# Seven-product matmuls of an fp32 macaron block: a merge with seven additions and a seeded PSUM bank, plain weight sums, one sum per block by an adding DMA, four quads in every gate/up block

## The chip, the cores and the metric

The kernel runs on one core of a Trainium2 chip. The metric is the device time in microseconds (us) of one execution; the number for a kernel is the median of its runs.

## The reference, cut to what matters

A block of width 2048 on 256 positions, all in fp32: half a feed-forward network (FFN1), a hybrid mixer (RWKV7 scan, pooling branch, gates), and half a second feed-forward network (FFN2), each with an RMS norm before and after. What the change touches is the two FFNs and, by the same functions, the mixer's last matmul.

```python
D_MODEL, SEQ, D_FF = 2048, 256, 5632      # D_FF = ceil(8 * 2048 / 3 / 256) * 256

def _swiglu(x, w_gate, w_up, w_down):
    return (jax.nn.silu(x @ w_gate) * (x @ w_up)) @ w_down
...
f = _swiglu(_rmsnorm(h, ln_ffn1_pre), ffn1_gate, ffn1_up, ffn1_down)
h = h + 0.5 * _rmsnorm(f, ln_ffn1_post)
mx = _hybrid_mixer(_rmsnorm(h, ln_mix_pre), ...)       # ends in m @ w_out
h = h + _rmsnorm(mx, ln_mix_post)
f = _swiglu(_rmsnorm(h, ln_ffn2_pre), ffn2_gate, ffn2_up, ffn2_down)
h = h + 0.5 * _rmsnorm(f, ln_ffn2_post)
```

## The kernel before, in words

**Precision.** A matmul in fp32 is made of three in fp32r: every operand is split into a high part (a cast on ACT) and a low part (the difference, on DVE), and `mm3` (L317) adds aH bH, aH bL and aL bH in one PSUM bank; its lines L319, L320, L321 are the three matmuls. The 256 positions are two halves h of 128, the weights come in tiles of 128 rows (k tiles) by 512 columns.

**A weight pair** (`fetch`, L362) is two k tiles: SP loads 512 KB into a w32 buffer, ACT casts it into a wH buffer of a ring of five (L373), DVE makes the low part wL (L383, 128 x 1024), PE uses it for 2 k tiles x 2 halves x 3 = 12 matmuls, and the ring buffer comes free.

**The seven-product scheme.** `seven` (L508) multiplies two weight blocks of 512 columns with the same activations: f and l are gate and up of the same columns, or two column blocks of down or of w_out. It takes a string of letters. `f` and `l` are a pair of that block. `q`, a quad, takes two k tiles of both blocks at once and makes the 2 x 2 products of them with seven multiplications in place of eight, so 21 matmuls for 24. For that, DVE makes sums of the raw weights: t13 (L576, 1024 wide), t2 (L581) and t4 (L585, 512 wide each), and four low parts (L598: three of 1024 and one of 512). The sums of the activations (S, L441 to L446) are made once per FFN and used by all blocks. The results collect in eight PSUM banks: f0, f1, l0, l1 (pool "mm", four buffers) also take the pairs' products; p1, p5, p6, p7 (pool "ms", four buffers) take only quads.

**The merge.** After a block's last quad ACT copies p1 into a buffer u0 (L640), and DVE makes u1 = p6 + u0, u2 = p7 + u1, u1 = p5 + u1 and u3 = p5 + u2, four additions of 512 that each read the one before or its neighbour (L645, `u<-ms`). When the f pairs are through, `close_f` adds f0 and f1 (L645, `u<-mm`), and at the block's end `total` (L693) adds l0 and l1: eight additions.

**The stages of an FFN.** `ffn` (L989) runs over 11 column blocks of gate and up. The first is multiplied without `seven`, the second with pairs only, and the other nine by turns with four quads ("ffqfqfqlqlll") and three ("fffqffqlqllll"): 32 quads. Silu of gate on ACT (L1067) times up on DVE (`mult`, L1074) gives the block of h, which DVE transposes in 32 x 32 pieces (L875), POOL moves by DMA (L892, `x<-T`), and ACT and DVE split into high and low (`carry`, L932; the lows are L909). Then `post` runs down: four column blocks in two calls of `seven`, the second of which holds back 16 k tiles of one block (TRAIL) and multiplies them at the end, first for one half of the positions, then for the other (`by_half`, L402). At the very end each half is squared and summed (in down by a custom DVE instruction, L1173, after `total`; in the mixer's w_out stage by ACT straight from the bank, L987), POOL takes the root (L1178), and DVE scales and adds the residual (L1182).

**The order.** The program writes the order of every engine by hand. A planner (`Plan.solve`, L137) places the operations with list scheduling: PE's sequence is given by the code; every operation has a due time, worked back from its first use on PE with planned latencies (LAT), and of those that can start first on an engine the one due first goes ahead. Loads may start at most FETCH = 22 us before they are due.

Of the kernel before, what the change touches and what calls it, by code (L numbers as in the profile page):

```python
# [47 lines left out]
GATE_UP = ["", "ffffffffllllllll"] + ["ffqfqfqlqlll", "fffqffqlqllll", "ffqfqfqlqlll", "fffqffqlqllll", "ffqfqfqlqlll", "fffqffqlqllll", "ffqfqfqlqlll", "fffqffqlqllll", "ffqfqfqlqlll"]  # L48
SUMS = (2, 2)
BY_DMA = range(0)  # L50
LAT = dict(PE=0.22, DVE=0.1, ACT=0.17, SP=0.0, POOL=8.0)
# [169 lines left out]
class Block:  # L221
# [95 lines left out]
    def mm3(s, ps, aH, aL, bH, bL, start, stop):  # L317
        nc = s.nc
        nc.tensor.matmul(ps, aH, bH, start=start, stop=False)  # L319
        nc.tensor.matmul(ps, aH, bL, start=False, stop=False)  # L320
        nc.tensor.matmul(ps, aL, bH, start=False, stop=stop)  # L321
# [99 lines left out]
    def sums(s, T, Td, j, out, own=None, nq=2, used=(), x32=None):  # L421
# [13 lines left out]
        def second():  # L435
            x = tt["x"] if x32 is None else x32[0][0].rearrange(
                "p (a b) t -> p a b t", b=2)[:, :nq]
            a11, a21 = x[:, :, 0, :P], x[:, :, 0, P:]
            a12, a22 = x[:, :, 1, :P], x[:, :, 1, P:]
            f = tt["f"] = s.unit((P, 4, nq, P), F32, "sf")  # L440
            V.scalar_tensor_tensor(out=f[:, 0], in0=a21, scalar=-1.0, in1=a22, op0=ALU.mult,  # L441
                                   op1=ALU.subtract)
            V.scalar_tensor_tensor(out=f[:, 1], in0=f[:, 0], scalar=-1.0, in1=a11,
                                   op0=ALU.mult, op1=ALU.subtract)
            V.tensor_tensor(out=f[:, 2], in0=a11, in1=a21, op=ALU.subtract)
            V.tensor_tensor(out=f[:, 3], in0=a12, in1=f[:, 1], op=ALU.subtract)  # L446
# [61 lines left out]
    def seven(s, wf, cf, wl, cl, at, dep, KT, need, sm, order, ev_f, ev_l, used, trail=0):  # L508
# [4 lines left out]
        n = order.count("q")  # L513
# [4 lines left out]
        left = dict(f0=std + n, f1=std, l0=std + n, l1=std + n, p1=n, p5=n, p6=n, p7=n)  # L518
# [9 lines left out]
        def mul(b, x, wt):  # L528
# [5 lines left out]
            s.mm3(bank[b], *x, *wt, new, left[b] == 0)  # L534
# [9 lines left out]
        def pair(k, w, c0, b, by_dma):  # L544
            low, dst = s.fetch(w, k, c0, keep, by_dma, by_dma)

            def do():
                for i in range(2):
                    for h in range(2):
                        mul(f"{b}{h}", rows(k + i, h), ws[k + i])  # L550
            d = p.pe(12 * MM, do, [low, dep(k)] + claim(b + "0", b + "1"), dst)
# [3 lines left out]
        def quad(q):  # L555
# [10 lines left out]
            def get(m):  # L566
                i, x_ = m // 2, "ab"[m % 2]
                if m < 2:
                    v[x_] = raw((ka, kb)[m])
                w, c0 = ((wl, cl), (wf, cf))[(m + i) % 2]  # L570
                nc.sync.dma_start(out=v[x_][:, i],
                                  in_=w[(k + i) * P:(k + i + 1) * P, c0:c0 + 512])

            def t13():
                v["t13"] = s.unit((P, 2, 512), F32, "t13")
                V.tensor_tensor(out=v["t13"], in0=v["a"],  # L576
                                in1=v["b"][:, :1].to_broadcast([P, 2, 512]), op=ALU.subtract)
# [6 lines left out]
            def t4():  # L584
                V.tensor_tensor(out=v["t24"][:, 1], in0=v["b"][:, 1], in1=v["t24"][:, 0],  # L585
                                op=ALU.subtract)
# [9 lines left out]
            def low(n_, m):  # L596
# [3 lines left out]
            ld = [p.op("SP", 0.4, lambda m=m: get(m), take=([ka], [kb], (), ())[m], size=0.26,  # L600
                       chain="SP", ahead=FETCH) for m in range(4)]

            def half(n_, m, deps, rel):
# [5 lines left out]
            n13 = p.op("DVE", two, t13, ld[:3], [k13, k24], [ka, kb])  # L609
            la, ra = half("a", 2, [ld[0], ld[2]], [ka])  # L610
            n2 = p.op("DVE", one, t2, [n13], (), [ka, k13])
# [7 lines left out]
                                  mul("f0", S_(4), x["a"][1])),  # L619
                 [la, ds, dep(k)] + claim("p1", "f0", "f1"), ra)  # L620
            p.pe(3 * MM, lambda: mul("l0", rows(k + 1, 0), x["b"][0]),
                 [lb] + claim("l0", "l1"), rb)
# [4 lines left out]
                                      mul("l1", rows(k + 1, 1), x["t24"][1])),  # L627
# [14 lines left out]
        def add(o, b, i):  # L642
            if u[o] is None:
                new(o)
            V.tensor_tensor(out=u[o], in0=bank[b], in1=u[i], op=ALU.add)  # L645
        m, use = {}, {}

        def merge(d):
            for i in range(4):
# [4 lines left out]
            for o, b, i in ((1, "p6", 0), (2, "p7", 1), (1, "p5", 1), (3, "p5", 2)):  # L654
                d = m[f"u{o}"] = p.op("DVE", one, lambda o=o, b=b, i=i: add(o, b, i),
                                      [d] + (use[o][0] if o > 1 or b == "p6" else []))
                held[b].append(d)
                use[i][1].append(d)
        nq, last = 0, {}
        ks = dict(f=iter(range(K0, KT, 2)), l=iter(range(K0, KT - trail, 2)))  # L660
        for c in order:
            if c == "q":
                last["q"] = quad(nq)
# [10 lines left out]
            if c == "f" and left["f"] == std // 2:  # L674
                m["f"] = last["f"]

                def close_f():
                    for h, i in ((0, 1), (1, 3)):
                        if n:
                            d = p.op("DVE", one, lambda h=h, i=i: add(i, f"f{h}", i),  # L680
                                     [last["f"], m[f"u{i}"], last["q"]])
# [5 lines left out]
                if not n or "u3" in m:  # L687
# [4 lines left out]
        def total(h):  # L692
            V.tensor_tensor(out=u[2 * h], in0=bank[f"l{h}"], in1=u[2 * h], op=ALU.add)  # L693
        if trail:
            def finish(h, d):
                d = p.op("DVE", one, lambda: total(h), [d, m["u0"], m["u3"]], due=p.clk)
                ev_l(h, d, lambda: u[2 * h], None)
            s.by_half(wl, cl, KT - trail, KT, lambda k, h: mul(f"l{h}", rows(k, h), ws[k]),
                      keep, finish, [dep(k) for k in range(KT - trail, KT, 4)],
                      used)  # L700
            return
        for h in range(2):
            if n:
                d = p.op("DVE", one, lambda h=h: total(h), [p.last, m["u0"], m["u3"]])
                held[f"l{h}"].append(d)
                ev_l(h, d, lambda h=h: u[2 * h], use[2 * h][1])
# [282 lines left out]
    def ffn(s, wg, wu, wd, uT, rs, gpost, resid, emit, reload, xs=None):  # L989
# [53 lines left out]
        su, sud, suk = [None] * 4, {}, []  # L1043
# [96 lines left out]
    def post(s, wd, at, KT, gpost, fac, resid, emit, reload, hT, hTd, sm, plan, hTk=None):  # L1140
# [8 lines left out]
        part, direct = [None, None], KT == NKD  # L1149
# [865 lines left out]
```

## Time and profile before

| | before |
|---|---|
| median of 3 runs | 2017.59 us (2016.92 to 2018.37) |
| span of the profiled execution | 2015.4 us |
| time of the profiled execution itself | not listed apart; the span is 2.2 us under the median |
| PE busy | 2000.9 us (99%) |
| DVE busy | 1824.7 us (91%) |
| ACT busy | 1192.3 us (59%) |
| POOL busy | 327.6 us (16%) |
| HBM read | 396.69 MB, 201 GB/s over the span |

The span is the time between the first and the last record of one execution under the profiler. A busy time adds the durations of an engine's instructions; matmuls overlap their neighbours (one lasts 0.39 us, the next starts 0.23 us after it), so that PE's rate is read from the distance of starts. A row of a timeline is start, length, engine, line, operation, output<-input, shapes and how many in a row; in square brackets stands how long the engine was idle before it, and for whom. A row of groups gives count, busy time, mean ns of one, and idle time before.

### The profile page before, as it was taken

The numbers are of one execution on the slowest core, as the hardware profiler recorded it, in microseconds if no ns is written. First come the engines' busy times: TensorE is split into PE (matmuls) and PEld (weight loads), VectorE is DVE, ScalarE is ACT, GpSimd is POOL, SyncE is SP. The second block draws the span as 40 slices with busy tenths as digits, with TensorE's granted clock in tenths as the row PEclk, the third lists the DMA queues.
The fourth block names the chain that finished last, engine by engine and source line by source line (L and its number), as shares of the span: only waits on it lengthen the run. The fifth ranks groups of instructions, "written<-read, shape, count | busy, mean of one in ns | idle before, by whom it ended". The sixth has DMA issues, their size and how long they took to land.

```text
span 2015.4 us, 28684 instructions
## 1 busy us (share of the span) xinstructions
PE 2000.9 (99%) x9957; PEld 1655.1 (82%) x9957; DVE 1824.7 (91%) x2424; ACT 1192.3 (59%) x1586; POOL 327.6 (16%) x673
## 2 busy tenths in 40 slices
PE   9999999999999999999999999999999999999997
PEld 7888888888888888888788788888888888888886
DVE  6999999999999957789689678979999999999997
ACT  7555665556666566685476434665656555566663
POOL 0111211131000123403220111011113111310000
PEclk9999999999999999999999999999999999999999
DMA  7675674667568577757456547666656747665683
GB/s 268 224 241 182 220 242 160 218 213 241 175 203 299 209 212 214 205 175 214 146 173 190 159 168 269 244 216 215 228 198 218 245 142 235 211 228 183 207 294 126
DMA packets 227419, 423.56 MB, mean 210 GB/s; under 512 B 24639, under 2 KB 28105, under 8 KB 227273
## 3 DMA queue, kind: packets, MB, share of 16 engines
q1 hardware_dynamic: 204713, 384.70, 57.9%
q0 software_dynamic: 22272, 36.51, 5.5%
q8 instruction: 78, 1.28, 0.3%
q10 hardware_dynamic: 288, 0.52, 0.1%
q14 instruction: 68, 0.56, 0.1%
HBM read 396.69 MB, written 8.39 MB: 201 GB/s over the span
## 4 chain that ended last, share of the span: by engine, by line
PE 97%; DVE 1%; issue 1%; DMA 0%; ACT 0%; POOLq 0%; POOL 0%; DVEq 0%; ACTq 0%
PE mm L319 27%; PE mm L321 26%; PE mm L320 26%; PE ms L320 5%; PE ms L321 5%; PE ms L319 5%; PE tr L849 1%; PE pA L1733 0%; DVE u L645 0%; PE mc L817 0%; DMA x<-in_x_dram 0%; PE pU L1829 0%; PE pSa L1841 0%; PE pY L1864 0%; PE pT L1900 0%
## 5 line engine op out<-in xcount | busy, mean ns | idle before, releaser
L319 PE MATMUL mm<-wH,xH 128*128 128x512 f32 (+1 forms) x2116 | 825.5, 391 | 0.0
L320 PE MATMUL mm<-wL,xH 128*128 128x512 f32 (+1 forms) x2116 | 821.2, 388 | 0.0
L321 PE MATMUL mm<-wH,xL 128*128 128x512 f32 (+1 forms) x2116 | 821.1, 388 | 0.0
L319 PEld LDWEIGHTS mm<-wH,xH 128*128 128x128 f32 x2116 | 397.4, 188 | 82.1
L321 PEld LDWEIGHTS mm<-wH,xL 128*128 128x128 f32 x2116 | 397.4, 188 | 82.0 <-DVE xL L867 0.2
L373 ACT CAST wH<-w 128x1024 fp32r<-128x1024 f32 x313 | 326.2, 1054 | 231.7 <-PE mm L321 208.1
L320 PEld LDWEIGHTS mm<-wL,xH 128*128 128x128 f32 x2116 | 397.7, 188 | 79.7
L383 DVE TENSOR_TENSOR wL<-w,wH 128x1024 fp32r<-128x1024 f32 x313 | 373.0, 1218 | 18.9 <-ACT wH L373 17.3
L593 ACT CAST wH<-t 128x1024 fp32r<-128x1024 f32 x208 | 219.4, 1055 | 217.0 <-PE mm L321 108.9
L296 DVE TENSOR_TENSOR wL<-w,wH 128x1024 fp32r<-128x1024 f32 (+2 forms) x200 | 236.6, 1192 | 95.7 <-ACT wH L295 94.1
L295 ACT CAST wH<-w 128x1024 fp32r<-128x1024 f32 (+2 forms) x200 | 205.4, 1034 | 170.9 <-PE mm L321 150.7
L892 POOL DMA_DIRECT2D x<-T x352 | 173.1, 499 | 729.8 <-DVE T L875 190.3
L598 DVE TENSOR_TENSOR wL<-t,wH 128x1024 fp32r<-128x1024 f32 x208 | 248.6, 1217 | 0.7 <-ACT wH L593 0.7
L593 ACT CAST wH<-w 128x1024 fp32r<-128x1024 f32 x208 | 168.3, 835 | 56.6 <-PE mm L321 30.0
L598 DVE TENSOR_TENSOR wL<-w,wH 128x1024 fp32r<-128x1024 f32 x208 | 194.5, 951 | 0.3
L576 DVE TENSOR_TENSOR t<-w,w 128x1024 f32<-128x1024 f32 x104 | 126.7, 1218 | 0.0
L320 PE MATMUL ms<-wL,sH 128*128 128x512 f32 x276 | 107.6, 390 | 0.2
L319 PE MATMUL ms<-wH,sH 128*128 128x512 f32 x276 | 107.4, 389 | 0.0
L321 PE MATMUL ms<-wH,sL 128*128 128x512 f32 x276 | 107.4, 389 | 0.0
L585 DVE TENSOR_TENSOR t<-w,t 128x512 f32<-128x512 f32 x104 | 71.8, 690 | 2.6
L581 DVE TENSOR_TENSOR t<-w,t 128x512 f32<-128x512 f32 x104 | 71.3, 686 | 0.6
L645 DVE TENSOR_TENSOR u<-ms,u 128x512 f32<-128x512 f32 x92 | 61.4, 686 | 1.4
(317 smaller groups left out, 2107.8 us busy)
## 6 DMA issues: line engine op xcount, KB each, us to landing
w<-in_w_in_dram SPq DMA_DIRECT2D x128, 512.0 KB
w<-in_ffn_up_dram SPq DMA_DIRECT2D x112, 512.0 KB
w<-in_ffn_gate_dram SPq DMA_DIRECT2D x110, 512.0 KB
w<-in_ffn_down_dram SPq DMA_DIRECT2D x104, 512.0 KB
w<-in_ffn_down_dram SPq DMA_DIRECT2D x144, 256.0 KB
w<-in_ffn_gate_dram SPq DMA_DIRECT2D x132, 256.0 KB
w<-in_ffn_up_dram SPq DMA_DIRECT2D x128, 256.0 KB
w<-in_w_out_dram SPq DMA_DIRECT2D x24, 512.0 KB
```

The costliest lines, as they stand in the source:

```text
L295: s.nc.scalar.copy(vH, v)
L296: s.nc.vector.tensor_tensor(out=vL, in0=v, in1=vH.bitcast(F32), op=ALU.subtract)
L319: nc.tensor.matmul(ps, aH, bH, start=start, stop=False)
L320: nc.tensor.matmul(ps, aH, bL, start=False, stop=False)
L321: nc.tensor.matmul(ps, aL, bH, start=False, stop=stop)
L373: nc.scalar.copy(x["H"], x["v"])
L383: nc.vector.tensor_tensor(out=x["L"], in0=x["v"], in1=x["H"].bitcast(F32), op=ALU.subtract)
L576: V.tensor_tensor(out=v["t13"], in0=v["a"], in1=v["b"][:, :1].to_broadcast([P, 2, 512]), op=ALU.subtract)
L585: V.tensor_tensor(out=v["t24"][:, 1], in0=v["b"][:, 1], in1=v["t24"][:, 0], op=ALU.subtract)
L593: nc.scalar.copy(H, src)
L598: V.tensor_tensor(out=L, in0=src, in1=H.bitcast(F32), op=ALU.subtract)
L892: nc.gpsimd.dma_start(out=x[0][q * 32:q * 32 + 32, i], in_=src[i * 32:i * 32 + 32, q])
```

## The change

- **Strings.** All nine blocks have "ffqqfQqfllll", so four quads: 36 per FFN. Down's and w_out's strings stay.
- **Plain sums.** The signs in the sums of weights and activations are chosen differently, so that t13 and t4 are additions, and the activations' sums are plain differences and one addition (tensor_tensor in place of scalar_tensor_tensor). Which product goes to which bank changes with them.
- **The adding DMA.** In the quad written `Q` (one per block, 18 in all) t13 is not made by DVE: SP loads two raw tiles into t13 (`begin`), and then one DMA from POOL's queue adds the up block's tile to both halves (`adding`, 512 KB written). The planner counts 20 us for it (FAR).
- **The merge.** In gate/up: u1 = p6 + u0, u2 = p7 + u1, then p5 - u2 is written straight into the bank l1 (`seed`), before any product has gone there; u1 = u1 - p5; two additions in `close_f`; `total` only for l0. l1's product with silu (L1130 now) works in place in its bank, and its transpose reads the bank. The first l pair is split: its six matmuls for the first half, then its six for the second, which wait for the seed (`ready`). A bank that DVE writes into between matmuls has the group check of the matmuls off (`skip_group_check`).
- **The end of down.** In the call with TRAIL, `into` adds u3 to the bank l1 and subtracts u1 from l0 before the 16 held-back k tiles, whose matmuls wait for that; `total` at the end is gone. The last norm always squares the bank on ACT (`direct = True`).

PE has 8852 instructions instead of 8876 (24 matmuls fewer), DVE 2269 in both, ACT 1417 for 1401, POOL 190 for 168, SP 999 for 965 in the written orders. On DVE the list between the seed of one gate/up block (L686, one per block) and the next block's holds about 23 instructions of 1024 elements and 24 of 512; from the first seed of an FFN to the sixth it holds 114 and 123, from the sixth to the ninth 69 and 69, and PE's list 900 and 540 matmuls.

The DVE order at the merge of a gate/up block in FFN1, before (L383 are weight lows; ms are the banks p6, p7, p5; the numbers tell the buffers apart):

```order
L383 TENSOR_TENSOR wL_576_2532<-w32_532_2333,wH_575_2531 128x1024
L645 TENSOR_TENSOR u_582_2558<-ms_541_2357,u_578_2551 128x512
L645 TENSOR_TENSOR u_584_2562<-ms_538_2349,u_582_2558 128x512
L645 TENSOR_TENSOR u_582_2558<-ms_537_2345,u_582_2558 128x512
L645 TENSOR_TENSOR u_587_2581<-ms_537_2345,u_584_2562 128x512
L383 TENSOR_TENSOR wL_580_2554<-w32_558_2441,wH_579_2553 128x1024
L645 TENSOR_TENSOR u_582_2558<-mm_513_2253,u_582_2558 128x512
L645 TENSOR_TENSOR u_587_2581<-mm_514_2257,u_587_2581 128x512
```

And the same place now (L385 are the weight lows, L681 additions, L686 the seed of bank l1, L677 the subtraction of p5):

```order
L385 TENSOR_TENSOR wL_496_2155<-w32_455_1981,wH_495_2154 128x1024
L681 TENSOR_TENSOR u_500_2176<-ms_457_1985,u_497_2170 128x512
L681 TENSOR_TENSOR u_504_2184<-ms_451_1967,u_500_2176 128x512
L686 TENSOR_TENSOR mm_505_2187<-ms_450_1963,u_504_2184 128x512
L385 TENSOR_TENSOR wL_499_2174<-w32_479_2090,wH_498_2173 128x1024
L677 TENSOR_TENSOR u_500_2176<-u_500_2176,ms_450_1963 128x512
L385 TENSOR_TENSOR wL_507_2196<-w32_480_2098,wH_506_2195 128x1024
L681 TENSOR_TENSOR u_497_2170<-mm_435_1893,u_497_2170 128x512
L681 TENSOR_TENSOR u_504_2184<-mm_436_1897,u_504_2184 128x512
```

The third instruction of the merge now writes into a bank, and a weight low stands between it and the one after it. On PE, 21 matmuls stand between the last one into p6 and the first that waits for the seed.

The DVE order before the held-back k tiles of FFN2's down, before (L1159 are products of finished columns with the gain):

```order
L1159 TENSOR_TENSOR fg_2603_13145<-u_3664_17948,gb_2599_13141 128x512
L645 TENSOR_TENSOR u_3858_18784<-ms_3693_18043,u_3855_18764 128x512
L383 TENSOR_TENSOR wL_3857_18781<-w32_3823_18618,wH_3856_18780 128x1024
L645 TENSOR_TENSOR u_3861_18796<-ms_3691_18036,u_3858_18784 128x512
L1159 TENSOR_TENSOR fg_2603_13145<-u_3665_17951,gb_2599_13141 128x512
L383 TENSOR_TENSOR wL_3860_18794<-w32_3836_18679,wH_3859_18793 128x1024
L383 TENSOR_TENSOR kL_3863_18800<-w32_3839_18684,kH_3862_18799 128x1024
L383 TENSOR_TENSOR kL_3865_18810<-w32_3840_18686,kH_3864_18809 128x1024
L645 TENSOR_TENSOR u_3858_18784<-ms_3690_18032,u_3858_18784 128x512
```

And now (L1215 are these products, L679 and L677 make u3 and u1, L689 is `into`):

```order
L681 TENSOR_TENSOR u_3886_18846<-ms_3721_18120,u_3883_18839 128x512
L1215 TENSOR_TENSOR fg_2618_13186<-u_3698_18032,gb_2614_13182 128x512
L681 TENSOR_TENSOR u_3887_18861<-ms_3717_18110,u_3886_18846 128x512
L679 TENSOR_TENSOR u_3890_18866<-ms_3716_18106,u_3887_18861 128x512
L677 TENSOR_TENSOR u_3886_18846<-u_3886_18846,ms_3716_18106 128x512
L385 TENSOR_TENSOR wL_3880_18814<-w32_3840_18644,wH_3879_18813 128x1024
L689 TENSOR_TENSOR mm_3730_18160<-mm_3730_18160,u_3890_18866 128x512
L689 TENSOR_TENSOR mm_3710_18086<-mm_3710_18086,u_3886_18846 128x512
```

The additions stand close together and end in two instructions in the banks themselves; between the last matmul into p6 and the first held-back one PE has 27 matmuls.

The diff, cut to its core:

```diff
+Q4 = "ffqqfQqfllll"
-GATE_UP = ["", "ffffffffllllllll"] + ["ffqfqfqlqlll", "fffqffqlqllll", ...]
+GATE_UP = ["", "ffffffffllllllll"] + [Q4] * 9
+FAR = 20.0
...
         def pair(k, w, c0, b, by_dma):
...
-            d = p.pe(12 * MM, do, [low, dep(k)] + claim(b + "0", b + "1"), dst)
+            deps = [low, dep(k)] + claim(b + "0", b + "1")
+            if b == "l" and ready:
+                p.pe(6 * MM, lambda: do((0,)), deps)
+                d = p.pe(6 * MM, lambda: do((1,)), ready, dst)
+            else:
+                d = p.pe(12 * MM, lambda: do((0, 1)), deps, dst)
...
+            def begin():
+                v["t13"] = s.unit((P, 2, 512), F32, "t13")
+                for i, (w, c0) in enumerate(((wf, cf), (wl, cl))):
+                    nc.sync.dma_start(out=v["t13"][:, i],
+                                      in_=w[(k + i) * P:(k + i + 1) * P, c0:c0 + 512])
+
+            def adding():
+                nc.gpsimd.dma_start(out=v["t13"], in_=wl[k * P:(k + 1) * P, cl:cl + 512]
+                                    .unsqueeze(1).to_broadcast([P, 2, 512]), accum_op=ALU.add)
...
+            if far:
+                n13 = p.op("SP", 0.8, begin, take=[k13], size=0.52, ahead=FETCH)
+                n13 = p.op("POOL", 1.0, adding, [n13], size=0.94, lat=FAR)
...
+        def seed():
+            bank["l1"] = s.pm.tile([P, 512], F32, tag="mm", name=s.nm("mm"))
+            V.tensor_tensor(out=bank["l1"], in0=bank["p5"], in1=u[2], op=ALU.subtract)
+
+        def into(h, i):
+            V.tensor_tensor(out=bank[f"l{h}"], in0=bank[f"l{h}"], in1=u[i],
+                            op=ALU.add if h else ALU.subtract)
...
-            for o, b, i in ((1, "p6", 0), (2, "p7", 1), (1, "p5", 1), (3, "p5", 2)):
+            for o, b, i in ((1, "p6", 0), (2, "p7", 1), (3, "p5", 2), (1, "p5", 1)):
+                if o == 3 and not early:
+                    d = p.op("DVE", one, seed, [d])
+                    ready.append(d)
...
+            if early and trail:
+                d = p.op("DVE", one, lambda: into(1, 3), [m["u3"]])
+                ready.append(d)
+            if trail:
+                d = p.op("DVE", one, lambda: into(0, 1), [m["u1"]])
+                ready.append(d)
...
-                      keep, finish, [dep(k) for k in range(KT - trail, KT, 4)],
-                      used)
+                      keep, lambda h, d: ev_l(h, d, lambda: bank[f"l{h}"], held[f"l{h}"]),
+                      [dep(k) for k in range(KT - trail, KT, 4)] + ready, used)
...
-        part, direct = [None, None], KT == NKD
+        part, direct = [None, None], True
```

114 lines of the change are left out of this document (66 added, 48 removed).

## The prediction

> **What bounds the kernel now.** I read the page's busy shares and its chain first, then what PE waited for, then two stretches of the gate/up stages by windows, and last the timelines of single blocks on DVE, ACT and PE. The page's head and its chain of the work that ended last:
>
> ```profile
> span 2015.4 us, 28684 instructions
> PE 2000.9 (99%) x9957; PEld 1655.1 (82%) x9957; DVE 1824.7 (91%) x2424; ACT 1192.3 (59%) x1586; POOL 327.6 (16%) x673
> ...
> PE 97%; DVE 1%; issue 1%; DMA 0%; ACT 0%; POOLq 0%; POOL 0%; DVEq 0%; ACTq 0%
> ```
>
> The waits of PE, whole list, and a stretch inside the gate/up blocks of each FFN (columns: stretch, length, then busy us and instruction count of PE, PEld, DVE, ACT, POOL, then granted clock, DMA share, GB/s):
>
> ```profile
> PE warm L725 <- POOL ident masks.py:199: 1.7, 1, 1.7
> PE tr L849 <- DMA x<-in_x_dram: 1.2, 1, 1.2
> PE pU L1829 <- DVE R L1854: 0.3, 1, 0.3
> ...
> 140.00:440.00 300.00, 300.00 (x1325) 248.39 (x1325) 296.89 (x340) 176.05 (x196) 55.00 (x112) 1.00 0.61 203
> 1400.00:1700.00 300.00, 300.00 (x1325) 248.47 (x1325) 296.21 (x342) 176.81 (x199) 55.01 (x112) 1.00 0.63 209
> ```
>
> PE is the bound: it has 97% of the chain and waits 3.2 us in all. In gate/up it starts 1325 matmuls in 300 us without a wait, 300 / 1325 = 0.2264 us each at a granted clock of 1.00. But DVE is busy 296.89 of the same 300 us. PE is ahead of a second bound by one per cent, and the change moves both.
>
> **What goes on PE.** Per FFN 36 quads instead of 32, 8 more in all. A quad takes 21 matmuls where two pairs take 24, and the orders of the two programs differ by exactly 24 matmuls: 24 x 0.2264 = **-5.4 us**, all on the chain as long as nobody keeps PE waiting.
>
> **What comes to DVE in gate/up.** The pitch of its instructions, from back-to-back groups on DVE at the merge of one block (start, length, operation; DVE has no gap here):
>
> ```profile
> 376.63 4.62 DVE L383 TENSOR_TENSOR wL<-w,wH 128x1024 fp32r<-128x1024 f32 x4
> 381.17 2.73 DVE L645 TENSOR_TENSOR u<-ms,u 128x512 f32<-128x512 f32 x4
> 383.82 1.28 DVE L645 TENSOR_TENSOR u<-mm,u 128x512 f32<-128x512 f32 x2
> ```
>
> Four of 1024 elements take 381.17 - 376.63 = 4.54 us, 1.135 each. Two independent ones of 512 take 1.28 together, and one alone is 0.68, so the pitch is 0.60; four that read each other's result take 2.73, 0.68 apart, 0.08 more per link; I take 0.10, since a link that waits for ACT or PE as well comes a little later. In the changed order the stretch of five blocks from the first seed of an FFN to the sixth holds 114 instructions of 1024 and 123 of 512, of which 30 read the one before: 114 x 1.135 + 123 x 0.60 + 30 x 0.10 = 129.4 + 73.8 + 3.0 = **206.2 us**. PE has 900 matmuls there: 900 x 0.2264 = **203.8 us**. DVE falls behind by about 2.4 us. In the next three blocks it has 69 and 69 (19 of them chained): 78.3 + 41.4 + 1.9 = 121.6 against 540 x 0.2264 = 122.3, so nothing is lost further. The reason is plain from the parts: a quad brings 6.4 us of DVE work and saves two lows of 1.135; 0.44 quads more per block are +2.84 - 1.0, the adding DMA takes off one t13 (-1.135) and the merge one addition (-0.6). That is +0.1 us of DVE per block, while PE loses 0.3. So DVE becomes the bound in gate/up, and what remains is how much of its debt is covered.
>
> **The seed as a new wait.** The second half of the first l pair (6 matmuls into l1) waits for the seed, and behind it on PE stands the rest of the block. Between the last matmul into p6 and that half lie 3 + 12 + 6 = 21 matmuls, 4.75 us. The seed needs ACT's copy of p1 and three chained DVE instructions, p6, p7 and the seed itself. When the merge started after p6's last matmul in two blocks of before (PE, ACT and DVE rows):
>
> ```profile
> 213.27 0.39 PE L321 MATMUL ms<-wH,sL 128*128 128x512 f32 x1
> 215.25 2.73 DVE L645 TENSOR_TENSOR u<-ms,u 128x512 f32<-128x512 f32 x4
> ...
> 377.83 0.39 PE L321 MATMUL ms<-wH,sL 128*128 128x512 f32 x1
> 378.71 0.57 ACT L640 COPY u<-ms 128x512 f32<-128x512 f32 x1
> ```
>
> From p6's end (213.66 and 378.22) to the first addition (215.25 and 381.17) it took 1.6 and 2.95 us; three chained ones take 2.1 more. The seed is there 3.7 to 5.05 us after p6, against a cover of 4.75: between 1.1 us to spare and 0.3 short, where DVE is on time, and 0.6 to spare as the middle. So DVE's 2.4 us of debt, less 0.6, come through to PE: about 1.8 us per FFN, **+3.6 us** for both. The bounds are 0 (the lows stand far enough ahead to pay all of it) and 3.3 per FFN (the debt, the 0.3 short, and 0.02 more for each of 30 links).
>
> **The trailing k tiles of down.** Here PE now waits for `into(1, 3)` and `into(0, 1)` before the last 16 k tiles of an FFN's down. The cover after p6 is 27 matmuls, 6.1 us. In FFN2 of before the copy and the first addition came so (PE, ACT, DVE):
>
> ```profile
> 1976.24 0.39 PE L321 MATMUL ms<-wH,sL 128*128 128x512 f32 x1
> 1978.30 0.58 ACT L640 COPY u<-ms 128x512 f32<-128x512 f32 x1
> 1981.77 0.68 DVE L645 TENSOR_TENSOR u<-ms,u 128x512 f32<-128x512 f32 x1
> ```
>
> Nothing was urgent there: the addition came 5.1 us after p6. Now DVE has, after the copy, in its order: p6, an fg product, p7, u3, u1, a low of 1024 and the two into; 7 x 0.60 + 1.135 and four links of 0.1 are 5.7 us after a copy that ends 1.1 to 2.25 us after p6's end (1976.63). That is 6.8 to 8.0 us against 6.1: 0.7 to 1.9, and 0 if the planner's copy comes as soon as the bank is full and the low is early. I take 0.8 each, **+1.6** for two FFNs, bounds 0 and 4. PE's queue stands still behind it, and nothing else is late, since DVE uses the time for lows.
>
> **The adding DMA.** No row of before shows one. The nearest are other 512 KB transfers from POOL's queue, plain ones (queue, count, KB, us from issue to landing):
>
> ```profile
> h<-hsp POOLq DMA_DIRECT2D x8, 512.0 KB, 6.2
> gb<-in_ln_ffn_post_dram POOLq DMA_DIRECT2D x4, 512.0 KB, 6.8
> xr<-in_x_dram POOLq DMA_DIRECT2D x4, 512.0 KB, 8.9
> x<-T POOLq DMA_DIRECT2D x352, 32.0 KB, 4.4
> ```
>
> If reading, adding and writing back doubles the longest, it lands after 18 us; the plan leaves it 20, and needs its sum only for the fourth step of the block. It stands on POOL's queue ahead of the 16 moves of x32 (L948) of a block; POOL is 16% busy, and their lows are due only in down. The two SP loads that fill t13 replace nothing (the raw tiles are still read), so 0.5 MB and the added 0.5 MB come on top at a DMA share of 0.61 to 0.63: hidden, 0 us. Without that cover each microsecond late is 18 us in all.
>
> **The end of the program.** Before, after the last matmul, on DVE and POOL; and the same step in OUT, where the bank was already squared by ACT directly:
>
> ```profile
> 1318.04 0.60 ACT L987 ACTIVATE junk<-mm 128x512 bf16<-128x512 f32 x1 [0.26 <-PE mm L321]
> 1318.54 0.20 ACT L987 ACTIVATION_READ_ACCUMULATOR junk<-mm 128x1 f32 x1
> 1319.71 0.20 DVE L1170 TENSOR_SCALAR rt<-ss,rp 128x1 f32<-128x1 f32 x1
> ...
> 2004.12 0.39 PE L321 MATMUL mm<-kH,xL 128*128 128x512 f32 x1
> 2004.54 0.69 DVE L693 TENSOR_TENSOR u<-mm,u 128x512 f32<-128x512 f32 x1 [5.59 <-PE mm L321]
> 2005.27 0.75 DVE L1173 CUSTOM_DVE_ANT_0 junk<-u,rp 128x512 bf16<-128x512 f32 x1
> 2006.12 0.92 POOL L1178 TENSOR_TENSOR rs<-rt,mhalf 128x1 f32<-128x1 f32 x1 [9.94 <-DVE rt L1173]
> ```
>
> From PE's end (2004.51) to POOL it was 1.6 us. By ACT it is 0.70 for the square with its accumulator and 0.20 on DVE, about 1.0 with the hand-overs: **-0.6 us**, once, since in FFN1 PE goes on. Bounds 0 and -0.8.
>
> The other edits cost nothing that counts: plain differences for the sums of the activations (L443 to L446, same width), and 16 casts of 512 more on ACT, at 59%.
>
> **The sum.** -5.4 + 3.6 + 1.6 - 0.6 = -0.8 us. Span 2015.4 and the median of the runs, 2017.59, differ by 2.2 us, and the profiled execution has no time of its own in the list; I put the difference on the median: **2016.8 us**. With all bounds: -6.2 to +5.2.
>
> **The rivals.** *First, all is covered.* Casts wait for a free ring buffer, that is for PE, more than for anything:
>
> ```profile
> ACT wH L373 <- PE mm L321: 208.1, 183, 1.8
> ...
> L645 DVE TENSOR_TENSOR u<-ms,u 128x512 f32<-128x512 f32 x92 | 61.4, 686 | 1.4
> L1074 DVE TENSOR_TENSOR u<-u,u 128x512 f32<-128x512 f32 x36 | 24.3, 681 | 0.0
> ```
>
> The first row shows weights standing ahead of PE at 183 casts, so a debt of 2.4 us that builds up over five blocks can be paid from what stands ahead. Against it: the order on DVE is fixed, and in it the seed sits behind lows that PE needs later. Then the time is 2017.6 - 5.4 - 0.6 = 2011.6, or 2013.2 with the wait in down. Chance 0.30.
>
> *Second, slower: DVE instructions on PSUM banks cost more.* The seed writes a bank, l1's product now works in place in it and the transpose reads it, each in every one of 18 blocks; before, no addition wrote to PSUM. As DVE is then the bound, each 0.1 us per block costs 1.8 us. From 0.27 us per block on (0.09 for each of the three) it takes 4.8 us more than my sum, 2021.6, and is slower than before by 4.0. The L645 and L1074 rows speak against dear reads: 686 ns with a source in PSUM, 681 with both in SBUF. Writing is not shown; by the longest 512-wide row above, 0.75 us, it would be 0.07 more. Chance 0.13.
>
> [...] Chance 0.05. [...]
>
> *Fourth, slower: the adding DMA comes late.* It decides where it lands over about 20 us after issue, since t13's low is then what PE waits for; 0.27 us late in each of 18 blocks is 4.9 us, 2021.7. For it: a read and a write per element on queues that carry 61% already. Chance 0.07.
>
> That the change doesn't do what it says is excluded for PE by the order (24 fewer). For DVE it partly holds: it has as many instructions as before.
>
> **How the numbers follow.** My own sum has 0.45. A difference of 0.2%, 4.0 us, is about the least that a measurement of this kernel can tell from none. Faster: the first rival, 0.30. Same: my sum and the third, 0.50; its own range is 2013.5 to 2021.6. Slower: the second and fourth, 0.20. The range reaches from the covered case, 2011.5, to 2022.5, and leaves out part of the slower cases.
>
> **What would show it.** In the changed profile: PE waits on DVE at L323 or L321 in gate/up, some 1.8 us per FFN, and DVE busy 99.5% or more there, fewer than 1325 matmuls in 300 us; PE's first matmul of the trailing tiles waiting under 1 us; the mean of the seed (L686) near 0.69 us; the adding DMA (L596) landing in under 18 us; POOL starting 1.0 us after the last matmul. If PE waits for nothing in gate/up, the debt was covered and I am wrong towards 2012; if it waits for t13's low, the DMA was late; if DVE's rows on PSUM are 0.75 us or more, the second rival holds.

## The result

The changed kernel takes 2027.73 us (median of 4 runs, 2025.32 to 2029.48), the kernel before 2017.28 beside it: a ratio of 1.0051, 95% interval 1.0038 to 1.0065. It is slower by 10.4 us, and lies over the top of the predicted range, 2022.5.

The page of the changed kernel, its head and its chain:

```profile
span 2025.6 us, 28825 instructions
PE 2002.2 (99%) x9933; PEld 1650.1 (81%) x9933; DVE 1824.4 (90%) x2424; ACT 1206.9 (60%) x1610; POOL 349.8 (17%) x691
...
PE 70%; DVE 18%; issue 5%; DMA 5%; ACT 0%; SPq 0%; DVEq 0%; POOLq 0%; POOL 0%; ACTq 0%
```

The busy shares are nearly what they were; the chain is not. It was PE at 97%, and now it runs through DVE for 18% of the span. The same two stretches of gate/up by windows, and the waits of PE:

```profile
140.00:440.00 300.00, 298.47 (x1311) 245.16 (x1310) 297.93 (x343) 181.40 (x202) 68.15 (x128) 1.00 0.70 224
1400.00:1700.00 300.00, 298.52 (x1311) 245.13 (x1310) 297.26 (x342) 181.80 (x202) 64.17 (x119) 1.00 0.70 226
```

```profile
PE mm L321 <- ACT kH L375: 4.2, 2, 2.1
PE mm L321 <- DVE mm L686: 2.4, 5, 0.8
...
PE mm L322 <- DVE wL L385: 1.0, 1, 1.0
```

In 300 us PE starts 1311 matmuls where it started 1325: 14 x 0.2264 = 3.2 us lost in each FFN, more than the 1.5 us that the busy time shows, since a matmul that waits for its bank or its weights is drawn long: 0.50 us for 0.39 in the row at 213.49 below, behind the seed, and as much for the one at 1968.77, behind a weight low. The first row of the waits names a cast into kH on ACT as what PE waited for. That cast ended 0.06 us after `into` on DVE, but the matmul that waited reads wH and not kH, and run 1, which takes `into` out, has no such wait: what PE waited for was `into`.

Where the time went, from the gaps between the starts of matmuls (all over 0.29 us, less 0.227 each, in the one profiled execution):

| | before | after | difference | forecast |
|---|---|---|---|---|
| 24 matmuls fewer | | | -5.4 | -5.4 |
| gate/up, first to last quad, both FFNs | 0 | 5.9 | +5.9 | +3.6 |
| before the held-back k tiles of down, both | 0 | 6.3 | +6.3 | +1.6 |
| weight lows late elsewhere in down and at its start | 0.8 | 2.0 | +1.2 | 0 |
| last matmul to the end of the program | 10.9 | 12.2 | +1.3 | -0.6 |
| start of the program, and the rest | | | +0.9 | 0 |
| sum | | | +10.2 | -0.8 |

**The seed.** One block of FFN1 in the changed kernel, PE, ACT and DVE rows (start, length):

```profile
206.75 4.62 DVE L385 TENSOR_TENSOR wL<-w,wH 128x1024 fp32r<-128x1024 f32 x4
...
208.16 0.39 PE L323 MATMUL ms<-wH,sL 128*128 128x512 f32 x1
...
208.86 0.57 ACT L671 COPY u<-ms 128x512 f32<-128x512 f32 x1
...
211.29 1.41 DVE L681 TENSOR_TENSOR u<-ms,u 128x512 f32<-128x512 f32 x2
...
212.73 0.70 DVE L686 TENSOR_TENSOR mm<-ms,u 128x512 f32<-128x512 f32 x1
...
213.49 0.50 PE L321 MATMUL mm<-wH,xH 128*128 128x512 f32 x1 [0.18 <-DVE mm L686]
```

p6 is complete at 208.55, ACT's copy at 209.43; but four weight lows stand ahead of the merge on DVE until 211.3, and PE needs the last two of them only after the half pair that waits for the seed (their pairs start at 214.98 and 217.70). The seed is done at 213.43, 4.9 us after p6, and the cover was 4.75. Over the 18 blocks it is done 3.96 to 5.50 us after p6. PE waits for it in three of the nine blocks of each FFN, 2.1 us together; the other 0.9 us per FFN are lost at lows of later blocks.

**The end of down.** In FFN1, the same engines:

```profile
669.61 0.39 PE L323 MATMUL ms<-wH,sL 128*128 128x512 f32 x1
...
670.20 1.22 DVE L385 TENSOR_TENSOR wL<-w,wH 128x1024 fp32r<-128x1024 f32 x1
...
670.54 0.57 ACT L671 COPY u<-ms 128x512 f32<-128x512 f32 x1
...
671.33 1.28 DVE L1215 TENSOR_TENSOR fg<-u,gb 128x512 f32<-128x512 f32 x2
672.54 0.69 DVE L681 TENSOR_TENSOR u<-ms,u 128x512 f32<-128x512 f32 x1
...
674.46 0.69 DVE L679 TENSOR_TENSOR u<-ms,u 128x512 f32<-128x512 f32 x1
675.06 0.68 DVE L677 TENSOR_TENSOR u<-u,ms 128x512 f32<-128x512 f32 x1
675.66 1.22 DVE L385 TENSOR_TENSOR wL<-w,wH 128x1024 fp32r<-128x1024 f32 x1
675.73 0.39 PE L323 MATMUL mm<-wH,xL 128*128 128x512 f32 x1
...
676.79 1.29 DVE L689 TENSOR_TENSOR mm<-mm,u 128x512 f32<-128x512 f32 x2
...
678.23 0.47 PE L321 MATMUL mm<-wH,xH 128*128 128x512 f32 x1 [2.11 <-ACT kH L375]
```

From p6's end, 670.0, to the end of the second `into`, 678.08, it takes 8.1 us against a cover of 6.1. ACT's copy is done at 671.1, but DVE comes to p6's addition only at 672.5: a low and two products with the gain stand ahead of it. From there the chain takes 5.5 us. PE starts at 678.23 and not at 675.96. In FFN2 it is the same, 8.1 us and 2.3 us of wait. In FFN1 PE is slower for a while after the wait, with nothing to wait for (by windows, columns as in the prediction):

```profile
679.00:683.00 4.00, 4.00 (x12) 3.17 (x11) 4.00 (x5) 1.05 (x2) 0.00 (x0) 0.57 0.43 116
683.00:690.00 7.00, 7.00 (x33) 5.78 (x32) 5.86 (x11) 1.34 (x4) 0.00 (x0) 1.00 0.64 205
```

The granted clock is 0.57 in these four microseconds (0.50 from 679.3 to 682.7), and seven matmuls stand 0.427 us apart instead of 0.227: with the two beside them 1.6 us more. After the equal wait in FFN2 this profile shows no such drop (1.00 from 1992 to 1996).

### The profile page after: what moved, and what is told of

The parts are those of the page before. It is cut to its first block, busy times and chain, and to the rows that moved or that the text cites. A ratio compares the mean times of both kernels' runs of the same rounds, so it can differ in the third digit from the quotient of the medians.

```text
span 2025.6 us, 28825 instructions
## 1 busy us (share of the span) xinstructions
PE 2002.2 (99%) x9933; PEld 1650.1 (81%) x9933; DVE 1824.4 (90%) x2424; ACT 1206.9 (60%) x1610; POOL 349.8 (17%) x691
## 4 chain that ended last, share of the span: by engine, by line
PE 70%; DVE 18%; issue 5%; DMA 5%; ACT 0%; SPq 0%; DVEq 0%; POOLq 0%; POOL 0%; ACTq 0%
PE mm L321 20%; PE mm L322 19%; PE mm L323 19%; DVE wL L623 6%; DVE wL L385 3%; PE ms L322 3%; PE ms L323 3%; PE ms L321 2%; DMA w<-in_ffn_gate_dram 2%; DVE t L601 2%; DMA w<-in_ffn_up_dram 2%; DVE t L610 1%; DVE t L606 1%; DVE u L681 1%; DMA w<-in_ffn_down_dram 1%
## 5 line engine op out<-in xcount | busy, mean ns | idle before, releaser
L321 PE MATMUL mm<-wH,xH 128*128 128x512 f32 (+1 forms) x2068 | 808.5, 392 | 6.8 <-ACT kH L375 4.2
L322 PE MATMUL mm<-wL,xH 128*128 128x512 f32 (+1 forms) x2068 | 803.8, 389 | 1.0 <-DVE wL L385 1.0
L323 PE MATMUL mm<-wH,xL 128*128 128x512 f32 (+1 forms) x2068 | 803.7, 389 | 0.0
L385 DVE TENSOR_TENSOR wL<-w,wH 128x1024 fp32r<-128x1024 f32 x297 | 355.6, 1219 | 17.0 <-ACT wH L375 15.6
L618 ACT CAST wH<-t 128x1024 fp32r<-128x1024 f32 x224 | 236.2, 1055 | 219.5 <-PE mm L323 108.0
L623 DVE TENSOR_TENSOR wL<-t,wH 128x1024 fp32r<-128x1024 f32 x224 | 265.1, 1216 | 1.9 <-ACT wH L618 1.4
L322 PE MATMUL ms<-wL,sH 128*128 128x512 f32 x300 | 117.4, 391 | 0.4 <-DVE wL L623 0.3
L601 DVE TENSOR_TENSOR t<-w,w 128x1024 f32<-128x1024 f32 x94 | 114.6, 1219 | 2.5 <-DMA w<-in_ffn_down_dram 2.5
L321 PE MATMUL ms<-wH,sH 128*128 128x512 f32 x300 | 116.8, 389 | 0.0
L610 DVE TENSOR_TENSOR t<-w,t 128x512 f32<-128x512 f32 x112 | 77.3, 690 | 2.7
L606 DVE TENSOR_TENSOR t<-w,t 128x512 f32<-128x512 f32 x112 | 76.8, 686 | 0.6
L322 PEld LDWEIGHTS ms<-wL,sH 128*128 128x128 f32 x300 | 56.3, 188 | 14.4 <-DVE wL L623 2.9
```

The costliest lines, as they stand in the source:

```text
L321: nc.tensor.matmul(ps, aH, bH, start=start, stop=False, skip_group_check=seeded)
L322: nc.tensor.matmul(ps, aH, bL, start=False, stop=False, skip_group_check=seeded)
L323: nc.tensor.matmul(ps, aL, bH, start=False, stop=stop, skip_group_check=seeded)
L385: nc.vector.tensor_tensor(out=x["L"], in0=x["v"], in1=x["H"].bitcast(F32), op=ALU.subtract)
L601: V.tensor_tensor(out=v["t13"], in0=v["a"], in1=v["b"][:, :1].to_broadcast([P, 2, 512]), op=ALU.add)
L618: nc.scalar.copy(H, src)
```

## The experiments

Two theories. W: the two new waits of PE are chains of instructions that are longer than the matmuls that cover them; give them cover and they are gone. D: DVE has become the bound, and a wait only shows it; what is taken away at one place comes back at another. A ratio is against the kernel before, timed on the same chip, with its 95% interval.

**1. The end of down undone.** No `into` and no bank read by the last square: `finish` adds u3 and subtracts u1 after the held-back k tiles, and `direct = KT == NKD`.

```diff
-            if early and trail:
-                d = p.op("DVE", one, lambda: into(1, 3), [m["u3"]])
...
-        part, direct = [None, None], True
+        part, direct = [None, None], KT == NKD
```

> The end of down is as before (no into, the two sums at the very end, the last square by the custom DVE instruction); all else is as in the changed kernel. Theory W (the waits are chains that are longer than their cover): the two waits of 2.3 us, the 2.0 us at the lower clock behind the first and some 1 us at the end of the program go, so 2027.7 - 7 = about 2021, with PE waits in gate/up as they were (3.0 us per FFN). Rival D (DVE has too much to do, and a wait only shows it): PE waits at weight lows of down instead, and the time stays over 2025.

2023.83 us, 1.0033 (1.0020 to 1.0046). The waits before the held-back tiles are gone, and no others come in down; gate/up is as it was. But the gain is 3.9 and not 7, and the waits of PE show why:

```profile
PE mm L321 <- DVE mm L682: 2.3, 5, 0.8
...
PE pA L1783 <- DVE R L1759: 1.2, 2, 1.1
PE pB L1802 <- DVE R L1794: 1.1, 2, 0.8
```

pA and pB are banks of the mixer, which the edit doesn't touch. Its DVE order is not written by hand but by a scheduler, and it came out otherwise in this build (about a dozen of its instructions stand in another place, between 866 and 905 us); from the first matmul into pA on, the mixer is 3.6 us longer. Runs 3 and 4 have that order too.

**2. More cover for the seed.**

```diff
-Q4 = "ffqqfQqfllll"
+Q4 = "fqqfQqffllll"
```

> The string of the gate/up blocks is fqqfQqffllll: the same quads and pairs, but 12 more matmuls (2.7 us) between the last one into p6 and the first that waits for the seed. Theory W: the waits for the seed, 2.1 us per FFN, go, and the time falls by 4 us to about 2023.5. Rival D: DVE's work per block is the same, so PE waits as long at weight lows, and the time stays within 1.5 us of 2027.7.

2028.53 us, 1.0056 (1.0041 to 1.0071): nothing gained. The wait for the seed is gone from the list, and others stand in its place:

```profile
PE mm L321 <- DVE mm L689: 3.9, 2, 2.0
PE ms L322 <- DVE wL L623: 3.2, 13, 0.4
```

PE now waits for lows of quads, 13 times, and the gaps between matmuls in gate/up add up to 8.9 us, where they were 5.9. In gate/up D holds.

**3. No seed.** `early = True`, so that u3 is made in a buffer and added to l1 at the block's end.

> No seed in gate/up: u3 is made in a buffer and added to l1 at the end of the block, so eight additions, no split of the l pair and no wait of PE for DVE there. DVE gets 0.6 us more per block, 10.8 us in all. Theory W: the 4.2 us of waits for the seed go and little comes back: about 2024. Rival D: the 10.8 us come through to PE less the waits that they replace: 2030 or more, with PE waiting at weight lows in gate/up.

2035.88 us, 1.0092 (1.0077 to 1.0107), 8.2 more than the changed kernel. The wait for the seed is gone, but from the first quad of gate/up to the first of down the two FFNs are 4.9 and 4.8 us longer, 9.7 in all for 10.8 us more of DVE's work. Some 3.3 of the 9.7 are not waits: once in each FFN the granted clock is 0.50 behind a wait for a low.

```profile
374.70:378.00 3.30, 3.30 (x9) 2.56 (x8) 3.30 (x4) 2.59 (x4) 2.81 (x6) 0.50 0.49 162
1692.30:1695.50 3.20, 3.19 (x8) 2.52 (x9) 3.20 (x3) 2.76 (x4) 3.20 (x7) 0.50 0.59 203
```

The mixer's order adds 3.5 us, and down is 4.2 shorter, with 1.7 us for each wait for `into`, no lowered clock there and fewer late lows. D in gate/up.

**4. Two adding DMAs per block.**

```diff
-Q4 = "ffqqfQqfllll"
+Q4 = "ffQqfQqfllll"
```

> Two adding DMAs per block instead of one (string ffQqfQqfllll): 1.135 us less for DVE in each of 18 blocks, and the cover of the seed is the same. Rival D: nearly all of the 5.9 us of waits in gate/up go: about 2022. Theory W: the seed's chain is as long as before, the gain is under 1.5 us: 2026 to 2028. If the transfers are in each other's way, PE waits at lows of t13 and it is slower than 2028.

2022.78 us, 1.0026 (1.0016 to 1.0037), with the slow mixer order in it. The windows of gate/up:

```profile
140.00:440.00 300.00, 300.00 (x1326) 248.47 (x1325) 293.30 (x339) 186.04 (x205) 81.15 (x142) 1.00 0.80 244
1400.00:1700.00 300.00, 300.00 (x1326) 248.47 (x1325) 294.26 (x342) 183.84 (x203) 75.41 (x129) 1.00 0.80 246
```

DVE falls from 297.9 to 293.3 us of 300, and PE starts 1326 matmuls (1325 before the change): all waits in gate/up are gone, with the seed's cover as it was. The seeds themselves are done earlier, 2.3 to 4.1 us after p6. D.

**5. No adding DMA** ("ffqqfqqfllll").

> No adding DMA: t13 of every quad is made on DVE (string ffqqfqqfllll), 1.135 us more for DVE in each of 18 blocks, 20.4 us in all, and 18 MB less to move. Theory D (in gate/up DVE is the bound, and its debt comes through to PE): 2027.7 + 17 to 20, about 2045. Rival W (only chains shorter or longer than their cover matter): within 3 us of 2027.7.

2048.93 us, 1.0158 (1.0143 to 1.0174). 20.4 us more work on DVE make the kernel 21.2 us longer than the changed one. That the two are so near is in part luck: from the first quad of gate/up to the first of down the two FFNs are 13.1 and 13.9 us longer, 27 in all, and the rest is 6 us shorter (4.1 of it in down, 1.5 in the closing DRAIN of run 12 below). So in gate/up DVE's work comes through to the time whole, and in this run more than whole; why more is open.

**6. Runs 1 and 4 together**, by chance with the mixer's good order.

> Two adding DMAs per block and the end of down as it was before the change, together; the mixer's DVE order is that of the kernel before. If the losses are what the separate runs show (5.9 us of waits in gate/up, some 7 us at the two ends of down) and nothing else, it is 2027.7 - 5.9 - 7.5 = about 2014, faster than before by 3. If the two get in each other's way, or the second adding DMA delays loads of down, 2017 or more.

2015.08 us, 0.9989 (0.9980 to 0.9998): the two losses add up, 12.7 us of the changed kernel's time, and it is 1.8 under the kernel before.

**7 and 8. Runs 4 and 1 with 16 us in the plan for an adding DMA** (`FAR = 16.0`), which gives back the mixer's good order.

> As the run with two adding DMAs per block, but the planner counts 16 us instead of 20 for one; by that the automatic order of DVE's instructions in the mixer is again that of the kernel before, where the run with 20 us had another. If that other order costs 3.6 us in the mixer (from the shift of the first to the last matmul into pA), the time is 2022.8 - 3.6 = 2019.2. If the 3.6 us have another cause (the end of down, the loads), it stays near 2022.8.

> As the run with the end of down undone and one adding DMA per block, but with 16 us in the plan instead of 20; the mixer's DVE order is that of the kernel before again. If the other order cost 3.6 us: 2023.8 - 3.6 = 2020.2, which puts the end of down at 7.5 us. If not, it stays near 2023.8 and the end of down is worth 3.9 us.

Run 7: 2022.15 us, 1.0025 (1.0015 to 1.0035), only 0.6 less. The mixer's waits are gone, but the other plan made the waits for `into` 2.3 us each (1.7 in run 4) and brought waits for lows; the runs reach from 2019.75 to 2024.87, and those over 2022 have a mean granted clock of 0.996 or 0.997, those under it 0.998 but for one. A drop of the clock behind the wait that comes in some executions and not in others would fit that, but only one execution has a profile (2021.08, without a drop, mean granted clock 0.998). Run 8: 2021.33 us, 1.0021 (1.0011 to 1.0031), 2.5 less than run 1. That the mixer's order costs is shown by its waits, there in runs 1, 3 and 4 and absent here. From the last quad of FFN1's down to the first of w_out the profile of run 8 is 3.6 us shorter than that of run 1, while gate/up is 2.2 longer, since the plan changed there as well. The profiled execution of run 8 took 2024.90 us, 3.6 over the median; in it the granted clock is 0.50 from 9 to 15.5 us, at the start of the program, where no `into` stands. So the clock can drop without that wait.

**9. Cover for `into`**, on run 7.

```diff
-        (2, "fqflqfqflqfqflqfqflqfqfqff", TRAIL))
+        (2, "fqflqfqflqfqflqfqflqqfqfff", TRAIL))
```

> As the run with two adding DMAs per block and 16 us in the plan, and the last quad of down's second string stands one pair earlier (...qqfqfff for ...qfqfqff): the same work, 12 more matmuls (2.7 us) between the last one into p6 and the first that waits for into. Theory W for this place (the chain of 8.1 us is longer than its cover of 6.1): both waits of 2.3 us and the lower clock that follows them in some executions go, 2022.2 - 5 to 7 = 2015 to 2017. Rival D for this place (DVE is the bound there as well): PE waits at weight lows of down instead, 2020 or more.

2019.16 us, 1.0010 (1.0001 to 1.0020), 3.0 less. The wait for `into` is gone (W at this place), but waits for lows came, 1.8 us in the first down and 2.3 in the second, 1.3 of each at the two quads in a row: in part D.

**10. ACT first at the end**, on run 9: DVE's product of the last bank depends on the last norm's operation.

```diff
-            m = p.op("DVE", cost("DVE", 512), lambda: scale(h, 3, ap()), [d], due=t + 1)
+            m = p.op("DVE", cost("DVE", 512), lambda: scale(h, 3, ap()), [n], due=t + 1)
```

> As the run before it, and at the very end DVE's product of the last bank with the gain waits until ACT has squared the bank, where in the changed kernel ACT waits for that product. If the two reads of the bank follow each other by order alone, POOL starts 1.0 us after the last matmul instead of 1.84, and the time falls by 0.8 us; if ACT is late for another reason, nothing changes. With all three this should be about 2014.5 to 2016, under the kernel before.

2017.22 us, 1.0003 (0.9994 to 1.0013). POOL starts 1.1 us after the last matmul instead of 1.8. The time is 1.9 us less than in run 9; 0.7 of it lies behind the last matmul, and the rest is not explained by the edit. In the changed kernel (PE, DVE, ACT, POOL):

```profile
2013.00 0.39 PE L323 MATMUL mm<-kH,xL 128*128 128x512 f32 x1
2013.43 0.69 DVE L1215 TENSOR_TENSOR fg<-mm,gb 128x512 f32<-128x512 f32 x1 [5.80 <-PE mm L323]
2014.21 0.60 ACT L1043 ACTIVATE junk<-mm 128x512 bf16<-128x512 f32 x1 [10.25 <-DVE fg L1215]
...
2015.23 0.54 POOL L1234 TENSOR_TENSOR rs<-rt,mhalf 128x1 f32<-128x1 f32 x1 [10.38 <-DVE rt L1226]
```

ACT waits for DVE, which only reads the same bank; the two readers were put one behind the other, the wrong one first.

**11. The quads of down spread** ("...qfqfqlqfqfff"), on run 10.

> As the run with the square on ACT first, but down's second string ends in ...qfqfqlqfqfff: the cover of into is the same 39 matmuls, while no two quads stand next to each other. If the 1.6 us of waits for weight lows in each down came from the two quads in a row, they go and the time is 2017.2 - 3 = about 2014; if they come from DVE's work in down as a whole, they stay and it is 2016.5 to 2018.

2018.86 us, 1.0007 (0.9997 to 1.0016). The waits at the two quads are gone, and a wait for `into` of 1.2 us per FFN is back, so PE loses as much in down as in run 10 (1.8 and 1.9 us, there 1.8 and 1.8). That fits DVE's work in down as the bound rather than the two quads. The 1.6 us more in the time do not come from down.

**12. Run 6 with 16 us in the plan.**

> As the run with two adding DMAs per block and the end of down as before the change, with 16 us in the plan instead of 20 for an adding DMA. POOL's closing DRAIN is 11.5 us as in that run, since it goes by the number of adding DMAs (8.2 us with none, 9.7 with 18, 11.1 with 36 in the runs so far, and 0.4 more with the old last square). If the plan's 20 us cost nothing, the time is the same, 2014.5 to 2015.5; if loads that start later ease the queue, the wait of 1.3 us for weight lows in FFN1 goes and it is 2014.

2015.57 us, 0.9992 (0.9982 to 1.0001), no difference to run 6 that can be told. But its profile has no long wait left, the last matmul starts at 1999.33 where it started at 2004.12 before: 4.8 of the 5.4 us are there. Of that 1.8 us arrive in the time, against 2017.36. The rest is in the closing DRAIN of POOL's queue. The row of it in the kernel before (ns shortest/median/longest, then first and last start):

```profile
L2010 POOLq DRAIN  x3: 46/98/8569, 2006.1 to 2015.2; - x3
```

In run 5, with no adding DMA:

```profile
L2066 POOLq DRAIN  x3: 46/98/8191, 2037.6 to 2046.3; - x3
```

In the changed kernel, with 18:

```profile
L2066 POOLq DRAIN  x3: 46/98/9660, 2015.2 to 2025.4; - x3
```

In run 12, with 36:

```profile
L2060 POOLq DRAIN  x3: 46/98/11511, 2001.3 to 2013.3; - x3
```

It starts with POOL's last instruction, the root of the last norm, and is 8.19, 9.66 and 11.13 us long (run 4) with 0, 18 and 36 adding DMAs: 1.47 us per 18, 82 ns for each. With the old last square it is 0.38 longer, 8.57 and 11.51, by as much as the root itself is longer there (0.92 us for 0.54). Whether the number of these DMAs counts or what they move is not told apart.

**13 and 14. POOL's last instruction moved away from the end**: the two roots of FFN2 on ACT and DVE, in run 12 and in the kernel before.

```diff
+        def square_root(r2):
+            nc.scalar.activation(out=r2, in_=r2, func=AF.Sqrt)
...
+                nc.vector.reciprocal(r, r2)
...
+            if fin:
+                n = p.op("ACT", 0.25, lambda: square_root(r2), [n], due=t + 0.55)
```

> The run with two adding DMAs per block, the end of down as before and 16 us in the plan; the last two roots (FFN2) are taken by ACT (Sqrt) and DVE (reciprocal) instead of POOL. POOL's last instruction is then a load some 20 us before the end, and its closing DRAIN (11.5 us) lies beside the last matmuls. If that DRAIN ends the program, the end comes some 3 to 4 us sooner: 2015.6 - 3.5 = about 2012. If something else holds the end, or the DRAIN waits for the others, nothing moves.

> The kernel before with the same two roots moved to ACT and DVE, nothing else. There SP's wait for the stores ends 1.2 us before POOL's DRAIN (2013.44 and 2014.65), so if the DRAIN ends the program the gain is 1.2 us and at most 0.5 more for the faster root: 2016.9 - 1.5 = about 2015.4. If not, 2016.9.

Run 13: 2010.56 us, 0.9966 (0.9953 to 0.9979). Run 14: 2015.40 us, 0.9991 (0.9981 to 1.0000). In run 13 the DRAIN is of 12.4 us, but it starts at 1970.7 and ends 16 us before the last matmul; SP's wait for the stores ends the program:

```profile
L2072 POOLq DRAIN  x3: 46/97/12412, 1970.7 to 2008.5; - x3
L2072 SPq DRAIN  x3: 7/7/7, 2007.9 to 2008.2; - x3
```

So it was the DRAIN that held the end: with it out of the way the best version is 5.0 us shorter and the kernel before 1.6, of which 0.3 is the faster root (from the last matmul's start to DVE's last four products 2.63 us in run 13, 2.96 before). Run 13 beats both kernels: four quads and the seeded merge, two adding DMAs per block, the old end of down.

## Why the prediction was wrong

**The matmuls** (-5.4): right. Run 12 shows 4.8 of it at the last matmul.

**Gate/up** (+3.6, bounds 0 and 6.6): the mechanism was right, the bound moves from PE to DVE (busy 297.9 of 300 us), and the size was off: 3.0 us of gaps per FFN in place of 1.8. The step that failed is the 0.6 us of slack that I took off DVE's debt. The seeds came 3.96 to 5.50 us after p6, and in three blocks of nine later than the cover of 4.75, because lows stand ahead of the merge on DVE; there was nothing to spare. Without that slack the sum gives 2.4; the last 0.6 us are not accounted for. Runs 2 to 5 show that the cover is not the point.

**The end of down** (+1.6, bounds 0 and 4): the step that failed most. The chain was worked out at 6.8 to 8.0 us against 6.1, and then 0.8 was taken, for a copy and a low that would be early. The copy was early, 1.1 us after p6, and from p6's addition on the chain took 5.5 us where 5.7 was worked out. What the sum left out is the time between the two: it let DVE begin when the copy ends, but DVE had a low and two products ahead of p6's addition and began 1.4 us later. So it is 8.1 us, 2.3 of wait, twice, just over the top of the worked range. Two more terms were put at nothing: the clock that drops behind a wait (1.6 us), and the lows that are late elsewhere in down (1.2 us), where the prediction said that nothing else is late. This trace shows the drop, from 1.00 to 0.50 and from 0.227 to 0.427 us from matmul to matmul, after one of two such pauses of 2.3 us.

**The adding DMA** (0): it landed in 7.6 us, well under the 18 us, and no wait in gate/up is put down to it (run 4 with two of them has none there). But it was not free: 82 ns each in the closing DRAIN, 1.5 us in all, on a path that I had followed only as far as POOL's root.

**The end of the program** (-0.6): DVE's product came ahead of ACT's square, so POOL started 1.84 us after the last matmul and not 1.0, which is 0.2 later than before. The DRAIN from there was 1.1 us longer: +1.3.

**The rivals.** The first (all covered) did not happen: DVE's debt was not paid from what stood ahead. The second (dear PSUM banks) is refuted by the groups of the changed kernel (mean ns at the end of the busy time):

```profile
L681 DVE TENSOR_TENSOR u<-ms,u 128x512 f32<-128x512 f32 x46 | 31.6, 687 | 0.7
...
L931 DVE STREAM_TRANSPOSE T<-u 128x512 f32<-128x512 f32 x18 | 12.6, 702 | 0.0
L686 DVE TENSOR_TENSOR mm<-ms,u 128x512 f32<-128x512 f32 x18 | 12.6, 700 | 0.6
L1130 DVE TENSOR_TENSOR u<-u,u 128x512 f32<-128x512 f32 x18 | 12.5, 693 | 0.6
L1130 DVE TENSOR_TENSOR mm<-mm,u 128x512 f32<-128x512 f32 x18 | 12.5, 693 | 0.0
L931 DVE STREAM_TRANSPOSE T<-mm 128x512 f32<-128x512 f32 x18 | 12.2, 679 | 0.0
```

Writing the bank costs 13 ns (700 for 687), where the second rival needs 90, the product in place nothing (693 for 693), and the transpose is 23 ns shorter from the bank (679 for 702). The third had 0.05 in the forecast for a fixed price of reading a bank; no run shows one, and the last two pairs show 0 and -23 ns. The fourth (a late DMA) did not happen: the adding DMAs landed in 6.0 to 9.6 us. The slower side came by the terms of the main sum, nearly all at or over their upper ends together, and not by a rival; the range had treated them as if they were independent, though gate/up and down hang on one thing: DVE has no time left.

## What to carry to other kernels

When a second engine is busy for 99% of a stage, as DVE was here (296.89 of 300 us), price a change by that engine's work in it, in full (20.4 us more came to 21.2 in run 5), and expect a wait that is covered at one place to come back at the next, as in run 2; take the upper end for each of its chains, since all of them were late together here, and start a chain where that engine comes free and not where its input is ready (1.4 us apart at the end of down). Follow the last path to the last record of the program, the closing DRAIN included, and where that DRAIN is what ends last, as here, move the last instruction of its queue away from the end (5.0 us in run 13, 1.6 in run 14). Compare the order of parts that the change doesn't touch, where a scheduler writes it: three of these builds lost time (3.6 us in run 1, 3.5 in run 3) in a mixer in which no line was changed.

## What the runs showed of the hardware

The closing DRAIN of POOL's queue takes 8.19 us in this program without adding DMAs (run 5), 9.66 with 18 (changed kernel) and 11.13 with 36 (run 4), 82 ns more for each, counted from the start of POOL's last instruction. It is about a microsecond longer where that instruction stands far from the end (12.41 us in run 13 and 11.51 in run 12, 9.61 in run 14 and 8.57 in the kernel before).

The drops of the granted clock that were found between the first quad and the last matmul are to 0.50. In FFN1 of the changed kernel the drop lasts 3.4 us (679.3 to 682.7) and came after a pause of PE of 2.3 us. In FFN2 of run 2 it came after a pause of 2.2 us, with seven matmuls 0.427 us apart from 1991.90 to 1994.89. In run 3, in both FFNs, it came after two pauses of 1.5 and 0.9 us close together, with the clock at 0.50 through the windows of 3.30 and 3.20 us above. It did not come after the equal pause of 2.3 us in FFN2 of the changed kernel (1.00 from 1992 to 1996), nor after the two such pauses in the profile of run 7. What decides is not shown.

DVE's 512-wide tensor_tensor instructions take the same time within 20 ns with all operands in SBUF (681 ns in L1074 of the kernel before, 693 in L1130 of the changed one), with a PSUM bank as a source (680 in L677, 691 in L679), and with a bank as source and destination (692 in L689, 700 in L686).
